# Seven block products in place of eight for the first MLP matrix, in three of four chunks of a decoder layer

## The chip, the cores and the metric

The kernel runs on one core of one Trainium2 chip. The metric is the device time of one execution in microseconds; the time before is the median of three runs. The engines are called by the profile's names: PE (TensorE, matmuls; PEld are its weight loads), DVE (VectorE), ACT (ScalarE), POOL (GpSimd) and SP (SyncE, which here only issues DMAs). DMAs are issued by SP, ACT or POOL, each in the order of its own queue.

## The reference

One decoder layer on 512 tokens of width 1024, in float32: a normalised input, a token mixer (gated linear attention and latent attention side by side, merged by gates and projected), a layer norm, an MLP of hidden width 4096 with squared ReLU, and a last layer norm. The change lies in the MLP and in what feeds it:

```python
h = layer_norm(x, ln_in_g, ln_in_b)
for l in range(DEPTH):          # DEPTH = 1
    mix = token_mixer(h, ...)
    h = layer_norm(DEEPNORM_ALPHA * h + mix, ln1_g[l], ln1_b[l])
    ff = jnp.square(jax.nn.relu(h @ w_ff1[l])) @ w_ff2[l]     # (512,1024)@(1024,4096), (512,4096)@(4096,1024)
    h = layer_norm(DEEPNORM_ALPHA * h + ff, ln2_g[l], ln2_b[l])
```

## The kernel before

**Precision.** Every large product is made of three matmuls. An operand is split into a high part in the matmul's own rounded format and a low part, the rest; the kernel adds high x high, high x low and low x high. A split is one ACT copy (the high part) and one DVE subtraction (the low part). Weights are split on the chip after loading: `pump` (lines 157 to 184) walks one list, `stream`, of weight tiles of 128 x 1024 in the order in which they are needed, issues their loads on SP two entries ahead and their splits (lines 180 and 181) one entry ahead, for the second MLP product two ahead.

**The MLP.** The hidden width is handled in four chunks (`FC`) of 1024. In each chunk the first product runs `gemm_fm` (lines 221 to 244) over blocks of hidden features: a weight block of 128 x 128 is stationary, 512 tokens move, over eight k blocks; in all 8 x 8 x 3 = 192 matmuls of 512 columns. In chunk 0 the first four feature blocks are done in two halves of 256 tokens, since the second half of the input is normalised later. `ev_h` (lines 1212 to 1224) takes the sums out of PSUM with a ReLU and a square on ACT and starts `win_hid` (lines 1104 to 1120), which makes the operands of the second product from a pair of feature blocks.

The second product, `win_f2` (lines 1122 to 1202), already uses the scheme of seven products (Strassen's in Winograd's form): both matrices are cut into quadrants, four sums of quadrants are formed on each side, and seven products of quadrants replace eight. In `WIN` (line 327) an item is a weight operand, a half of its k blocks and a phase 0 to 6; each item is 12 matmuls of 512 columns, so a chunk has 14 x 12 = 168. The weight operands are quadrants "11", "21", "22" and the sums T1 = 12 - 11, T3 = 22 - 12, T2 = T3 + 11 and T4 = T2 - 21. `win_load` (line 1077) loads the quadrants of `w_ff2` through POOL's queue; `win_sums` (line 1086) makes T1, T3 and T2 on DVE, and T4 is made on DVE at line 1153. After the last item of a phase ACT copies the two banks out (line 1163), and POOL issues DMAs that add them to the residual rows in SBUF (line 1165). In chunk 3 the last six items run in another order, with their results added by DVE and the last layer norm following.

**Buffers and order.** Most tiles of 4 KB a partition share one pool `A` with 24 buffers; residual rows, T1 and T2 share eight others (tag C); `whi`/`wlo` have two each and `wraw` three; 2 KB tiles share pool `B` with 22. PSUM has four banks each in `pm` and `px`. The program is written as one main line with generators beside it (`spawn`, `tick`, `finish`), which are advanced between groups of matmuls. A scheduler then sets the order within each engine's queue by its own timing model; an engine runs its queue strictly in order, and a new tile waits until an old one of its pool is no longer used.

The input of the MLP is made by `ln_transpose` (lines 360 to 378): PE transposes, ACT writes the high part, DVE a temporary in pool `B` (line 368) and the low part. The result `h1T` is eight pairs of tiles (high, low) of 128 features x 512 tokens.

Of the kernel before, what the change touches and what calls it, by code (L numbers as in the profile page):

```python
# [10 lines left out]
F32 = mybir.dt.float32  # L11
# [5 lines left out]
ALU = mybir.AluOpType  # L17
# [35 lines left out]
def tile_hybrid_block(ctx: ExitStack, tc: tile.TileContext, I, out, dbg=None):  # L53
# [5 lines left out]
    sm = ctx.enter_context(tc.tile_pool(name="sm", bufs=4))  # L59
    pm = ctx.enter_context(tc.tile_pool(name="pm", bufs=4, space=bass.MemoryType.PSUM))  # L60
    px = ctx.enter_context(tc.tile_pool(name="px", bufs=4, space=bass.MemoryType.PSUM))

    uid = [0]
# [12 lines left out]
    def B(shape, dt=F32, n="b"):  # L76
        return pb.tile(shape, dt, tag="B", name=nm(n))
# [54 lines left out]


    stream = []
    st = {"dma": 0, "spl": 0, "gates": ()}
# [60 lines left out]
    def spawn(g):  # L196
        active.append(g)
        return g
# [122 lines left out]


    FC = 4
    F1 = [((0, 4), (4, 2), (6, 2))] + [tuple((b, 2) for b in range(0, 8, 2))] * 3
# [8 lines left out]
    fb = 0  # L333
    for ci in range(FC):
        nb = 8
        for b, w in F1[ci]:
            PL["f1", ci, b] = plan("w_ff1", (fb + b) * P, w * P, res=(ci == 0 and b == 0), per=8 // w)
        PL["f2", ci] = []
        for n, (op, hf, _) in enumerate(win_items(ci)):
            PL["f2", ci].append(len(stream))  # L340
            stream.append({"src": lambda q=(ci, op, hf): WQ[q], "nk": 2, "n": T, "res": False,
                           "ahead": 2, "home": "r" if ci == FC - 1 and n == 12 else HOMES[n]})
        fb += nb


    def ln_rows(src, dst, mv, on_act=False):
# [13 lines left out]
    def ln_transpose(rows, g, b, outs, hf, alt=False, n="h0"):  # L360
        tk = slice(hf * 256, (hf + 1) * 256)
        for k in range(NK):
            if len(outs) <= k:
                outs.append(A([P, 2, T], F32R, n) if n == "h0" else (B([P, T], F32R, n), B([P, T], F32R, n)))
            p = MM() if alt and k in (4, 5) else PX()
            for i in range(2):
                nc.tensor.transpose(p[:, i * P:(i + 1) * P], rows[2 * hf + i][:, k * P:(k + 1) * P], ident)
            tmp = B([P, 256], F32, "lnt")
# [9 lines left out]
            yield hd  # L378

    mvin = consts.tile([P, NT, 2], F32, name="mvin")  # L380
    hT = []

# [635 lines left out]
    finish(t_ln)  # L1018
    st["gates"] = st["ln"]
    t_ln = spawn(ln1(1))  # L1020
    accs = gemm_fm(PL["f1", 0, 0], h1T, T, None, toks=slice(0, 256))
    finish(t_ln)

    def residual1():
# [49 lines left out]
                nc.sync.dma_start(rows[:, c], r[:, c])  # L1074
        yield

    def win_load(ci):
        w2 = I["w_ff2"].rearrange("(k p) n -> p k n", p=P)
        for op, i, j in (("12", 0, 1), ("11", 0, 0), ("22", 1, 1), ("21", 1, 0)):
            for hf in range(2):  # L1080
                t = A([P, 2, T], F32, "wq")
                k0 = 8 * ci + 4 * hf + i
                nc.gpsimd.dma_start(t, w2[:, k0:k0 + 3:2, j * T:(j + 1) * T])
                WQ[ci, op, hf] = t

    def win_sums(ci):
        def held(*a, **kw):
            with ExitStack() as gates:
                if "ev" in st:
                    gates.enter_context(tc.issue_after(st["ev"].ins))  # L1090
                vtt(*a, **kw)
        for hf in range(2):
            q12 = WQ.pop((ci, "12", hf))
            t1 = WQ[ci, "T1", hf] = A([P, 2, T], F32, "T1")
            held(t1, q12, WQ[ci, "11", hf], op=ALU.subtract)
            yield
            held(q12, WQ[ci, "22", hf], q12, op=ALU.subtract)
            WQ[ci, "T3", hf] = q12
            yield
            t2 = WQ[ci, "T2", hf] = A([P, 2, T], F32, "T2")  # L1100
            held(t2, q12, WQ[ci, "11", hf], op=ALU.add)
            yield

    def win_hid(R, ops):
        a11, a12, a21, a22 = R[:, 0, :256], R[:, 1, :256], R[:, 0, 256:], R[:, 1, 256:]
# [16 lines left out]
    def win_f2(ci, hid):  # L1122
# [20 lines left out]
            return o  # L1143

        for n, (op, hf, ph) in enumerate(items[:8] if end else items):
            pump(PL["f2", ci][n])
# [4 lines left out]
            if n in (5, 6):  # L1151
                t2, q21 = WT.pop((ci, n - 5))
                vtt(t2, t2, q21, op=ALU.subtract)
                WQ[ci, "T4", n - 5] = t2
            if end and n == 6:
                gb.extend([bcast_row("ln2_g"), bcast_row("ln2_b")])
                for tt in range(3):
                    nc.sync.dma_start(out[tt * P:(tt + 1) * P, :], gb[1])
            if hf == 1:
                for t in range(2):  # L1160
                    o = bank[{3: 0, 6: 0, 5: 2}.get(ph, ph), t]
                    e = B([P, T], F32, "ev")
                    st["ev"] = act(e, o, AF.Copy, scale=-1.0 if ph == 4 else 1.0)  # L1163
                    for tt, j in (((0, 0),), ((0, 0),), ((2, 1),), ((0, 1),), ((2, 0),), ((0, 1),), ((2, 0), (2, 1)))[ph]:
                        nc.gpsimd.dma_start(res[tt + t][:, j * T:(j + 1) * T], e, accum_op=ALU.add)  # L1165
            if n == 9 and not end:
                win_load(ci + 1)
        if not end:
            return

# [31 lines left out]
        finish(spawn(ln2(3, bst)))  # L1202

    gb = []
    WQ, WT = {}, {}
    for ci in range(FC):
        nb = 8
        hid = []
        if ci == 0:
            win_load(0)  # L1210

        def ev_h(a, ps):
            r = B([P, T], F32, "relu")
            act(r, ps, AF.Relu)  # L1214
            if a % 2 == 0:
                hid.append({"R": A([P, 2, T], F32, "hr")})
            ops = hid[-1]
            R = ops["R"]
            act(R[:, a % 2, :], r, AF.Square)
            if a % 2:  # L1220
                h1 = A([P, 2, 2, 256], F32R, "h1p")
                split(R[:, :, :256], h1[:, 0], h1[:, 1])
                ops[0], ops[1] = [(h1[:, 0, i], h1[:, 1, i]) for i in range(2)]
                spawn(win_hid(R, ops))
        for b, w in F1[ci]:
            if ci == 0 and b == 0:
                gemm_fm(PL["f1", ci, b], h1T, T, ev_h, toks=slice(256, T), accs=accs)
                t_r1 = spawn(residual1())
            else:
                gemm_fm(PL["f1", ci, b], h1T, w * P, ev_h, width=2)  # L1230
            if b == 0:
                t_ws = spawn(win_sums(ci))
        if ci == 0:
            finish(t_r1)
        finish(t_ws)
        for hf in range(2):
            WT[ci, hf] = (WQ[ci, "T2", hf], WQ[ci, "21", hf])
        win_f2(ci, hid)


# [46 lines left out]
```

## Time and profile before

| what | value |
|---|---|
| time, median of 3 runs | 903.64 us (902.91 to 904.17) |
| span of the profiled execution | 901.4 us |
| instructions | 11,728 |
| PE matmuls | 4,472 |
| bytes moved by DMA | 101.47 MB |

The profiled execution is one of its own beside the three runs; the profile gives its span, from the first to the last instruction. Busy times are by engine, and the page's list of costliest groups merges instructions of one line. A matmul's duration in the list (389 ns for 512 columns) contains its latency, in which the next one already runs; how often matmuls follow one another is read from a window's length and their number.

### The profile page before, as it was taken

The page shows a single profiled execution, that of the slowest core. Times are in us where ns is not written, and L with a number is a line of the kernel's source. Part 1 is how long each engine was busy: PE and PEld are TensorE (multiplying, and loading weights), DVE is VectorE, ACT ScalarE, POOL GpSimd, SP SyncE. Part 2 cuts the span into 40 slices and gives each one's busy share as a digit, 9 for nine tenths or more (in the row PEclk, how much of TensorE's full clock was granted, in tenths as well). Part 3 has the DMA queues.
Part 4 walks back from the last instruction along what each step waited for, and adds up shares of the span by engine and source line. Part 5 has one row for each costly group of instructions (what it writes and reads, how often), then busy time and mean ns, then how long its engine had stood idle before and what let it go on. Part 6 is the DMA issues. An engine that isn't in the chain of part 4 may idle for free.

```text
span 901.4 us, 11728 instructions
## 1 busy us (share of the span) xinstructions
PE 878.1 (97%) x4472; PEld 746.5 (83%) x4472; DVE 566.1 (63%) x919; ACT 439.8 (49%) x745; POOL 172.8 (19%) x203
## 2 busy tenths in 40 slices
PE   5999999999999999999999999999999999999994
PEld 5988888888888888888888888988888888888883
DVE  7835855575635244657756797997557656754666
ACT  5555443444434333435645423366357546645654
POOL 1003442442511010000000002104400520241032
PEclk9999999999999999999999999999999999999997
DMA  7413213212213332212207618005940990397084
GB/s 243 122 47 94 90 52 94 71 47 71 75 38 93 88 105 74 68 42 65 94 24 260 205 49 303 2 0 139 302 120 25 261 249 25 80 312 169 1 210 94
DMA packets 63335, 101.47 MB, mean 113 GB/s; under 512 B 7680, under 2 KB 31616, under 8 KB 63280
## 3 DMA queue, kind: packets, MB, share of 16 engines
q1 hardware_dynamic: 48256, 64.04, 22.7%
q0 software_dynamic: 13104, 33.04, 15.2%
q10 hardware_dynamic: 1920, 3.66, 1.2%
q8 instruction: 35, 0.57, 0.3%
q14 instruction: 20, 0.16, 0.1%
HBM read 82.36 MB, written 3.67 MB: 95 GB/s over the span
## 4 chain that ended last, share of the span: by engine, by line
PE 92%; DMA 2%; ACT 2%; POOL 1%; issue 1%; DVE 1%; POOLq 0%; DVEq 0%; ACTq 0%
PE mm L231 16%; PE mm L233 15%; PE mm L232 15%; PE mm L264 6%; PE mm L265 6%; PE mm L266 6%; PE px L1141 3%; PE px L1140 3%; PE px L1142 3%; PE mm L1141 2%; PE mm L1140 2%; PE mm L1142 2%; PE px L680 2%; DMA res<-ev 1%; PE px L837 1%
## 5 line engine op out<-in xcount | busy, mean ns | idle before, releaser
L181 DVE TENSOR_TENSOR wlo<-wraw,whi 128x1024 fp32r<-128x1024 f32 (+1 forms) x104 | 117.7, 1132 | 162.3 <-ACT whi L180 154.9
L231 PE MATMUL mm<-h,whi 128*128 128x512 f32 x416 | 162.6, 392 | 0.4 <-ACT gt L924 0.4
L232 PE MATMUL mm<-h,whi 128*128 128x512 f32 x416 | 162.4, 390 | 0.0
L180 ACT ACTIVATE whi<-wraw 128x1024 fp32r<-128x1024 f32 (+1 forms) x104 | 100.3, 964 | 118.7 <-PE mm L232 68.3
L233 PE MATMUL mm<-h,wlo 128*128 128x512 f32 x416 | 154.9, 390 | 0.0
L1165 POOL DMA_DIRECT2D res<-ev x56 | 48.6, 980 | 238.2 <-ACT ev L1163 195.8
L231 PEld LDWEIGHTS mm<-h,whi 128*128 128x128 f32 x416 | 78.1, 188 | 16.3 <-ACT gt L924 0.6
L233 PEld LDWEIGHTS mm<-h,wlo 128*128 128x128 f32 x416 | 77.9, 188 | 16.4 <-DVE wlo L181 0.3
L232 PEld LDWEIGHTS mm<-h,whi 128*128 128x128 f32 x416 | 78.2, 188 | 15.6
L265 PE MATMUL mm<-wlo,h 128*128 128x512 f32 x128 | 50.3, 393 | 0.0
L266 PE MATMUL mm<-whi,h 128*128 128x512 f32 x128 | 50.1, 392 | 0.0
L264 PE MATMUL mm<-whi,h 128*128 128x512 f32 x128 | 49.7, 403 | 0.0
L1214 ACT ACTIVATE relu<-mm 128x512 f32<-128x512 f32 x32 | 18.8, 595 | 56.8 <-PE mm L233 56.8
L352 POOL TENSOR_TENSOR mv<-mv,mhalf 128x1 f32<-128x1 f32 x4 | 4.6, 1154 | 211.7 <-DVE mv L351 211.7
L619 POOL TENSOR_TENSOR rp<-rp 128x256 f32<-128x256 f32 x32 | 31.4, 983 | 60.9 <-ACT E L624 44.1
L626 DVE TENSOR_TENSOR M<-E,qk 128x512 f32<-128x512 f32 x32 | 27.3, 853 | 16.5 <-ACT E L624 16.5
L624 ACT ACTIVATE E<-rp 128x512 f32<-128x512 f32 x32 | 20.4, 638 | 26.9 <-POOL rp L620 26.9
L180 ACT ACTIVATE xh<-wraw 128x1024 fp32r<-128x1024 f32 (+1 forms) x20 | 19.0, 959 | 24.7 <-PE mm L266 16.0
L181 DVE TENSOR_TENSOR wlo<-wq,whi 128x1024 fp32r<-128x1024 f32 x15 | 18.4, 1223 | 19.7 <-ACT whi L180 19.7
L620 POOL TENSOR_TENSOR rp<-rp 128x256 f32<-128x256 f32 x32 | 27.5, 860 | 10.3 <-ACT q L649 8.1
L266 PEld LDWEIGHTS mm<-whi,h 128*128 128x128 f32 x128 | 24.0, 188 | 5.0
L265 PEld LDWEIGHTS mm<-wlo,h 128*128 128x128 f32 x128 | 24.1, 188 | 4.3
(383 smaller groups left out, 2240.9 us busy)
## 6 DMA issues: line engine op xcount, KB each, us to landing
wraw<-in_w_in_dram SPq DMA_DIRECT2D x40, 512.0 KB, 3.5
wraw<-in_w_ff_dram SPq DMA_DIRECT2D x32, 512.0 KB, 7.6
wq<-in_w_ff_dram POOLq DMA_DIRECT2D x32, 512.0 KB, 9.4
res<-ev POOLq DMA_DIRECT2D x56, 256.0 KB, 8.3
wraw<-in_w_o_gla_dram SPq DMA_DIRECT2D x8, 512.0 KB, 3.7
wraw<-in_w_o_mla_dram SPq DMA_DIRECT2D x8, 512.0 KB, 3.2
wraw<-in_w_out_dram SPq DMA_DIRECT2D x8, 512.0 KB, 4.3
wraw<-in_w_in_dram SPq DMA_DIRECT2D x8, 360.0 KB, 5.1
```

The source lines that it names most:

```text
L180: st["ins"] = act(hi[:, :nk, :n], raw[:, :nk, :n], AF.Copy)
L181: vtt(lo[:, :nk, :n], raw[:, :nk, :n], f(hi[:, :nk, :n]), op=ALU.subtract)
L231: mm(o, hi[:, c], xh, start=first, stop=False)
L232: mm(o, hi[:, c], xl, start=False, stop=False)
L233: mm(o, lo[:, c], xh, start=False, stop=last)
L264: mm(o, xh, hi[:, :n], start=opens, stop=False, skip_group_check=share)
L265: mm(o, xh, lo[:, :n], start=False, stop=False, skip_group_check=share)
L266: mm(o, xl, hi[:, :n], start=False, stop=last, skip_group_check=share)
L1140: mm(o, xh[:, c], hi[:, pp, cols], start=opens, stop=False, skip_group_check=True)
L1141: mm(o, xh[:, c], lo[:, pp, cols], start=False, stop=False, skip_group_check=True)
L1142: mm(o, xl[:, c], hi[:, pp, cols], start=False, stop=hf == 1 and pp == 1, skip_group_check=True)
L1165: nc.gpsimd.dma_start(res[tt + t][:, j * T:(j + 1) * T], e, accum_op=ALU.add)
```

## The change

The first product of chunks 1 to 3 is made by the same scheme of seven products. The weight `w_ff1` of a chunk is cut in quadrants by k and by features, the input in quadrants by k and by tokens. Where the second product's weight pieces had been taken in every other k block, chunks 1 to 3 now take them in the order in which the first product leaves the hidden features.

- `win_f1` (new) runs 14 items in the order 11, T1, T2, 21, T3, 22, T4, each of 24 matmuls of 256 columns, with weights stationary and tokens moving. Three pairs of banks hold the sums; in between ACT copies them to four tiles `R` (`copy`), DVE adds (`add`), and ACT applies ReLU and square to whole quadrants (`relu2`, `tail`). `put` splits quadrants into operands for the second product; `tail` forms their four sums. Two of the operands are written over parts of `h1T` that are no longer read.
- `sums_h1` (new) forms the four sums of the input's quadrants once, during the second product of chunk 0, and splits them; they stay in eight tiles. For this `ln_transpose` keeps its temporaries in tiles of 128 x 1024 and SP stores them to DRAM (`H1D`), from where they are read again.
- `load` replaces `win_load` after chunk 0 and issues all weight quadrants on SP; `hooks` places loads and sums at given items.
- `wsum` makes the weight sums, T2 and T4 in place. T1 and T3 of the first product stay on DVE; T2 and T4 of the first product and all four of the second go to POOL (`gtt`), each a tensor of 128 x 1024. Chunk 0 keeps its own on DVE, without the wait for an evacuation that `held` gave them.
- Splits of weight tiles go round three places (`"rww"`), for the first product two items ahead as well.

```diff
-    TAG_C = ('h0', 'qn', 'PT1', 'res', 'bc', 'T1', 'T2')
+    TAG_C = ('h0', 'qn', 'PT1', 'res', 'bc', 'T1', 'T2', 'w21')
...
+    WIN1 = tuple((op, hf, ph) for op, ph in (("11", 0), ("T1", 2), ("T2", 3), ("21", 1), ("T3", 6), ("22", 5), ("T4", 4))
+                 for hf in range(2))
...
+                home = "rww"[st["ring"] % 3] if u != ("f2", FC - 1) or n < 8 else "wawara"[n - 8]
...
+            if n == "h1":
+                if k % 4 == 0:
+                    raw = A([P, 4, 256], F32, "h1r")
+                tmp = raw[:, k % 4]
+            else:
+                tmp = B([P, 256], F32, "lnt")
...
+                if k % 4 == 3:
+                    H1D[hf, k // 4] = dr.tile([P, 4, 256], F32, name=nm("h1d"))
+                    nc.sync.dma_start(H1D[hf, k // 4], raw)
...
-                nc.gpsimd.dma_start(t, w2[:, k0:k0 + 3:2, j * T:(j + 1) * T])
+        (eng or nc.sync).dma_start(t, src[:, :, c0 + j * T:c0 + (j + 1) * T])
...
+    def wsum(u, op, hf, tt=None):
+        tt = tt or vtt
+        if op == "T1":
+            t = WQ[u, "T1", hf] = A([P, 2, T], F32, "T1")
+            tt(t, WQ[u, "12", hf], WQ[u, "11", hf], op=ALU.subtract)
...
+    for ci in range(1, FC):
+        u, v = ("f1", ci), ("f2", ci - 1)
+        for n, op, hf in ((6, "11", 0), (7, "11", 1), (8, "12", 0), (9, "12", 1), (10, "22", 0), (11, "22", 1)):
+            at(v, n, load, u, op, hf)
+        for hf in range(2):
+            at(u, 1 + hf, load, u, "21", hf)
+            at(v, 12 + hf, wsum, u, "T1", hf)
+            at(u, hf, wsum, u, "T3", hf)
+            at(u, 2 + hf, wsum, u, "T2", hf, gtt)
+            at(u, 6 + hf, wsum, u, "T4", hf, gtt)
+        v = ("f2", ci)
...
+        for hf in range(2):
+            at(u, 12 + hf, wsum, v, "T1", hf, gtt)
+            at(v, hf, wsum, v, "T3", hf, gtt)
+            at(v, 3 + hf, wsum, v, "T2", hf, gtt)
+            at(v, 5 + hf, wsum, v, "T4", hf, gtt)
...
+    def sums_h1():
+        q = {}
+        for i, j in ((1, 0), (1, 1), (0, 0), (0, 1)):
+            q[i, j] = A([P, 4, 256], F32, "h1q")
+            nc.sync.dma_start(q[i, j], H1D[i, j])
+        yield
...
+        vtt(q[1, 1], q[1, 0], q[1, 1], op=ALU.add)
+        yield
+        put(2, q[1, 1])
...
+    def win_f1(ci, hid):
...
+            for pp in range(2):
+                k = 2 * hf + pp
+                xh, xl = x(ph, k, 0), x(ph, k, 1)
+                for m in range(4):
...
+                    mm(o, hi[:, pp, c], xh, start=first, stop=False, skip_group_check=True)
+                    mm(o, hi[:, pp, c], xl, start=False, stop=False, skip_group_check=True)
+                    mm(o, lo[:, pp, c], xh, start=False, stop=k == 3, skip_group_check=True)
+                tick(4)
...
+        def tail():
+            for t in range(2):
+                r = R[2][:, 2 * t:2 * t + 2]
+                act(r, bank[0, t].rearrange("p (a b) -> p a b", b=256), AF.Relu)
+                act(r, r, AF.Square)
+                yield
...
+            s1 = A([P, 4, 256], F32, "hr")
+            vtt(s1, R[2], R[3], op=ALU.add)
+            put(2, s1)
...
+    at(("f2", 0), 7, lambda: spawn(sums_h1()))
+    win_f2(0, hid)
+    for ci in range(1, FC):
+        hid = [{} for _ in range(4)]
+        win_f1(ci, hid)
         win_f2(ci, hid)
```

More of the change, by code (lines that the diff above doesn't have):

```diff
@@ L323, in tile_hybrid_block @@
     FC = 4
-    F1 = [((0, 4), (4, 2), (6, 2))] + [tuple((b, 2) for b in range(0, 8, 2))] * 3
+    F1 = ((0, 4), (4, 2), (6, 2))
     HOMES = "wwrawarawawawa"
@@ L1075, in ln2 @@
         yield
-    def win_load(ci):
-        w2 = I["w_ff2"].rearrange("(k p) n -> p k n", p=P)
-        for op, i, j in (("12", 0, 1), ("11", 0, 0), ("22", 1, 1), ("21", 1, 0)):
-            for hf in range(2):
-                t = A([P, 2, T], F32, "wq")
-                k0 = 8 * ci + 4 * hf + i
-                nc.gpsimd.dma_start(t, w2[:, k0:k0 + 3:2, j * T:(j + 1) * T])
[L1084 to L1091, printed above, removed]
+    WQ = {}
@@ new lines, in load @@
+    def load(u, op, hf, eng=None):
+        what, ci = u
+        i, j = int(op[0]) - 1, int(op[1]) - 1
+        t = A([P, 2, T], F32, "w21" if op == "21" and ci else "wq")
+        if what == "f1":
+            src, c0 = I["w_ff1"].rearrange("(k p) n -> p k n", p=P)[:, 4 * i + 2 * hf:4 * i + 2 * hf + 2], 8 * ci * P
+        else:
+            w2 = I["w_ff2"].rearrange("(k p) n -> p k n", p=P)
+            k0 = 8 * ci + (4 * i + 2 * hf if ci else 4 * hf + i)
+            src, c0 = w2[:, k0:k0 + 2] if ci else w2[:, k0:k0 + 3:2], 0
+        (eng or nc.sync).dma_start(t, src[:, :, c0 + j * T:c0 + (j + 1) * T])
+        WQ[u, op, hf] = t
@@ L1092, in win_sums, with at, hooks, win_load0 @@
+    HOOKS = {}
+    def at(u, n, fn, *args):
+        HOOKS.setdefault((u, n), []).append((fn, args))
+    def hooks(u, n):
+        for fn, args in HOOKS.pop((u, n), ()):
+            fn(*args)
+    def win_load0():
+        for op in ("12", "11", "22", "21"):
+            for hf in range(2):
+                load(("f2", 0), op, hf, nc.gpsimd)
+    def win_sums0():
+        u = ("f2", 0)
         for hf in range(2):
-            q12 = WQ.pop((ci, "12", hf))
-            t1 = WQ[ci, "T1", hf] = A([P, 2, T], F32, "T1")
@@ L1204, in tile_hybrid_block, with ev_h @@
     gb = []
[L1205 to L1237, printed above, removed]
+    hid = []
+    win_load0()
+    def ev_h(a, ps):
+        r = B([P, T], F32, "relu")
+        act(r, ps, AF.Relu)
+        if a % 2 == 0:
+            hid.append({"R": A([P, 2, T], F32, "hr")})
+        ops = hid[-1]
+        R = ops["R"]
+        act(R[:, a % 2, :], r, AF.Square)
+        if a % 2:
+            h1 = A([P, 2, 2, 256], F32R, "h1p")
+            split(R[:, :, :256], h1[:, 0], h1[:, 1])
+            ops[0], ops[1] = [(h1[:, 0, i], h1[:, 1, i]) for i in range(2)]
+            spawn(win_hid(R, ops))
+    for b, w in F1:
+        if b == 0:
+            gemm_fm(PL["f1", b], h1T, T, ev_h, toks=slice(256, T), accs=accs)
+            t_r1 = spawn(residual1())
+            t_ws = spawn(win_sums0())
+        else:
+            gemm_fm(PL["f1", b], h1T, w * P, ev_h, width=2)
+    finish(t_r1)
+    finish(t_ws)
+    at(("f2", 0), 7, lambda: spawn(sums_h1()))
+    win_f2(0, hid)
+    for ci in range(1, FC):
+        hid = [{} for _ in range(4)]
+        win_f1(ci, hid)
         win_f2(ci, hid)
```

171 lines of the change are left out of this document (146 added, 25 removed).

## The prediction

> **What bounds the kernel now.** I read the page first, then stretches of time cut where the MLP's loops begin and end (taken from the lines of the matmuls), then the groups by line and shape, then POOL in order of time.
>
> ```profile
> PE 878.1 (97%) x4472; PEld 746.5 (83%) x4472; DVE 566.1 (63%) x919; ACT 439.8 (49%) x745; POOL 172.8 (19%) x203
> ...
> PE 92%; DMA 2%; ACT 2%; POOL 1%; issue 1%; DVE 1%; POOLq 0%; DVEq 0%; ACTq 0%
> ```
>
> PE is busy 97% of the span and carries 92% of the chain that ended last. The windows of the MLP (time, then busy us and instructions of PE, PEld, DVE, ACT, POOL, clock, DMA share, GB/s) alternate between second product and first product, from the second product of chunk 0:
>
> ```profile
> 605.33:643.41 38.08, 38.08 (x170) 31.54 (x169) 28.22 (x29) 23.04 (x32) 14.50 (x18) 1.00 0.68 196
> 643.41:686.93 43.52, 43.52 (x194) 36.05 (x193) 22.77 (x31) 23.07 (x34) 5.18 (x6) 1.00 0.51 119
> 686.93:725.01 38.08, 38.08 (x170) 31.54 (x169) 27.01 (x27) 21.95 (x31) 14.40 (x18) 1.00 0.70 198
> 725.01:768.53 43.52, 43.52 (x194) 36.05 (x193) 22.93 (x31) 23.81 (x35) 5.15 (x6) 1.00 0.50 117
> 768.53:806.61 38.08, 38.08 (x170) 31.54 (x169) 27.24 (x28) 23.27 (x32) 14.39 (x18) 1.00 0.72 203
> 806.61:850.13 43.52, 43.52 (x194) 36.05 (x193) 22.71 (x31) 22.47 (x33) 5.17 (x6) 1.00 0.48 113
> ```
>
> PE never pauses, at the full granted clock of 1.00. A first product of 192 matmuls of 512 columns takes 43.52 us (0.2267 each), a second of 168 takes 38.08; a chunk takes 81.6. DVE has a third of each window to spare, POOL two thirds. So a gain has to come from fewer PE columns, and it lasts only while the other engines keep up.
>
> **PE's new count.** Seven products of four k blocks, four feature blocks and three passes are 7 x 4 x 4 x 3 = 336 matmuls of 256 columns in place of 192 of 512: 86,016 columns for 98,304. The trace has such matmuls in the first stage of chunk 0:
>
> ```profile
> 558.50:568.50 10.00, 10.00 (x86) 1.00 0.43 151
> ...
> 575.30:586.00 10.70, 10.70 (x82) 10.29 (x81) 10.67 (x14) 3.87 (x8) 0.00 (x0) 1.00 0.01 2
> ```
>
> In the first row (PE alone) 86 matmuls, the outermost two in part, lie in 10.00 us: 0.116 to 0.119. In the second, all engines, 82 lie in 10.70: 0.130, with DVE busy for all but 0.03 us and PE now and then behind it. I take 0.120. So 336 x 0.120 = 40.3 us: 3.2 us less per first product, not the 5.4 that an eighth of 43.52 would be; at 0.116 it is -4.5, at 0.130 +0.2. Three chunks: -9.6. That is the whole expected gain. Chunk 0's first product stays.
>
> **What DVE and ACT pay.** Rows by line and shape, from the second product of chunk 0 to the last:
>
> ```profile
> L181 DVE TENSOR_TENSOR wlo<-wraw,whi 128x1024 fp32r<-128x1024 f32 x24 | 29.4, 1225 | 48.0 <-ACT whi L180 48.0
> ...
> L1091 DVE TENSOR_TENSOR T<-wq,wq 128x1024 f32<-128x1024 f32 x12 | 14.4, 1220 | 0.9 <-DMA wq<-in_w_ff_dram 0.9
> ...
> L107 DVE TENSOR_TENSOR h1p<-hr,h1p 128x512 fp32r<-128x512 f32 x12 | 8.2, 684 | 0.0
> ...
> L107 DVE TENSOR_TENSOR a<-hr,a 128x256 fp32r<-128x256 f32 x12 | 5.0, 418 | 0.0
> L180 ACT ACTIVATE whi<-wraw 128x1024 fp32r<-128x1024 f32 x26 | 27.4, 1055 | 10.1 <-PE mm L1142 5.7 <-PE mm L232 4.1
> L1163 ACT ACTIVATE ev<-px 128x512 f32<-128x512 f32 x30 | 17.3, 596 | 17.2 <-DMA res<-ev 11.6 <-PE px L1142 2.7 <-PE mm L1142 2.6
> ```
>
> A full-tile two-input DVE operation costs 1.22 us, a half tile 0.68, a quarter 0.42; a full-tile ACT pass 1.055.
> First product, changed chunk, DVE: 14 low parts of weights (8 before) 17.1; two T3 sums 2.4; the split of the first quadrant 4 x 0.42 = 1.7 and of the second 1.2; six additions from PSUM 4.1. Sum 26.5 of 40.3 us.
> Second product, DVE: 14 low parts 17.1; two T1 sums of the next chunk 2.4; four hidden sums of `tail` 4.9; four full-tile splits 4.9 and one in quarters 1.7. Sum 31.0 of 38.1. The old splits and sums of `win_hid` go away.
> ACT per chunk: 28 weight passes 29.5, 18 full tiles' worth of copies, ReLU, squares and high parts about 19, 14 evacuations of 0.6: 58 of 78.4 us. It stays below PE, as does DVE by itself.
>
> **What POOL pays, and what that costs DVE.** Per changed chunk POOL does twelve 128x1024 sums: T2, T4 and the next product's T1 (two halves each) in the first product, T3, T2 and T4 in the second. The trace has none of 1024 columns. The nearest are these, with the two DVE operations beside them (first the instructions of a line with min/median/max in ns, then rows of the timeline):
>
> ```profile
> L535 POOL TENSOR_TENSOR g<-g,az x4: 1298/1307/2343, 66.7 to 71.5; 128x512 f32<-128x512 f32 x4
> L620 POOL TENSOR_TENSOR rp<-rp x32: 613/760/1605, 97.6 to 250.6; 128x256 f32<-128x256 f32 x32
> 66.67 6.11 POOL L535 TENSOR_TENSOR g<-g,az 128x512 f32<-128x512 f32 x4 [40.71 <-ACT az L532]
> 69.14 1.23 DVE L181 TENSOR_TENSOR wlo<-wraw,whi 128x1024 fp32r<-128x1024 f32 x1 [6.57 <-ACT whi L180]
> 71.53 2.33 DVE L181 TENSOR_TENSOR wlo<-wraw,whi 128x1024 fp32r<-128x1024 f32 x1 [1.17 <-ACT whi L180]
> ```
>
> Undisturbed, 256 columns take 0.61 and 512 take 1.30, so 1024 take 1.30 + 2 x 0.69 = 2.67, or 2.60 as two of 512. I take 2.6. The last rows matter more. Four POOL operations of 1.30 would be 5.2 us; they took 6.11, since one of them took 2.34 while a DVE subtraction ran; and the next subtraction took 2.33 where it takes 1.23, over the last 1.1-1.2 us of the fourth POOL operation. They ran one after the other, whichever came first, not side by side. So a POOL sum isn't taken off DVE: where DVE has two SBUF operands, it holds DVE for 2.6 us in place of the 1.22 that DVE itself would need.
>
> The Trainium skill has this as a rule (SBUF — State Buffer, "SBUF: two separate sides"): the port pair that DVE and GpSimd share is an exclusive lock kept for a whole instruction, also against DVE operations with two SBUF inputs. The trace agrees by the 2.33 us. By the Trainium skill's GPSIMD Engine Reference, section 3.1 (4497 ns for 2048 columns), a sum would be an estimated 2.25 us, which would take about 2 us off each second product's excess below.
>
> So DVE's two-SBUF work and POOL's sums are added (PSUM additions may lie beside a POOL sum):
> First product: 22.4 + 6 x 2.6 = 38.0 of 40.3 us: fits, barely.
> Second product: 31.0 + 15.6 = 46.6 of 38.1 us: 8.5 too long. Weights are split at most two items ahead (5.4 us), so little can be moved out. Bounds: nothing, if POOL's sums only fall in DVE's pauses, to +8.5 plus what imperfect packing adds. That DVE can be packed shows here:
>
> ```profile
> 557.70:568.70 11.00, 11.00 (x93) 10.95 (x93) 10.89 (x21) 2.13 (x3) 3.12 (x2) 1.00 0.47 165
> ```
>
> 10.89 of 11.00 busy. I add 1.0 per chunk for packing (bounds 0 and 4, about 5% of 86).
>
> **POOL's queue.** POOL still issues 14 accumulating DMAs per chunk, in order, and a sum behind one that waits is late. POOL by time, at the end of a second product and in the next:
>
> ```profile
> 646.71 0.84 POOL L1165 DMA_DIRECT2D res<-ev  x1 [6.64 <-DMA res<-ev]
> 648.42 4.34 POOL L1165 DMA_DIRECT2D res<-ev  x5 [0.87 <-DMA res<-ev]
> 695.95 1.72 POOL L1165 DMA_DIRECT2D res<-ev  x2 [43.19 <-ACT ev L1163]
> 702.32 0.84 POOL L1165 DMA_DIRECT2D res<-ev  x1 [4.65 <-ACT ev L1163]
> 703.63 0.85 POOL L1165 DMA_DIRECT2D res<-ev  x1 [0.48 <-DVE wlo L181]
> ...
> 728.62 1.72 POOL L1165 DMA_DIRECT2D res<-ev  x2 [7.17 <-DMA res<-ev]
> ```
>
> The last accumulations of a second product left 3.6 to 5.3 us into the next first product (728.62 and 730.34 less 725.01), those of the one before until 9.35 us into it (648.42 + 4.34 - 643.41). T2 is queued behind them. Its second half would be ready 5.3 + 2 x (2.6 + 1.22) = 12.9 or 17.0 us in, with one DVE operation before each; item 5 begins 5 x 2.88 = 14.4 in and needs ACT's and DVE's 2.3 us before, so 12.1. That is 0.8 to 4.9 late; I take 2.5 per chunk.
>
> **The rest.** Chunk 0's second product gets four sums and four splits of the hidden input (`sums_h1`: 8 x 1.22 = 9.8 DVE, 4.2 ACT), with its 28.22 DVE about 38.0 of 38.08; T1 replaces sums that stood there. Two of them can slip into the next chunk. I take +2 (0 to +6, if half doesn't fit). The `w_ff2` loads move from POOL's queue to SP's, eight per chunk, so SP issues 16 loads a chunk, in order; a load that waits for a buffer holds up the `w_ff1` quadrants behind it. The input's way to DRAM and back is four stores and four reads of 512 KB, covered by the DMA shares of 0.5 to 0.7 and by being issued seven items ahead; a load of that size lands in 7.6 us:
>
> ```profile
> wraw<-in_w_ff_dram SPq DMA_DIRECT2D x32, 512.0 KB, 7.6
> ```
>
> Without that cover a product waits for such a landing. I cost it at nothing (0 to +4). In the LN stage only the buffer of the temporary changes (0 to +2).
>
> **Sum.** Chunks 1 and 2: -3.2 + 2.5 + 8.5 + 1.0 = +8.8 each. Chunk 3 has no next T1 (8.5 - 2.4 = 6.1), and about 7 us of PE follow its last split, which I let cover 2: -3.2 + 2.5 + 4.1 = +3.4. Chunk 0: +2. In all 17.6 + 3.4 + 2 = +23.0 on the profiled span of 901.4: 924.4. The median of the runs, 903.64, lies 2.2 above that span, so 926.6, say 926.
>
> **The rivals.**
> *PE's count decides* (chance 0.14): POOL's sums mostly fall where DVE waits for ACT (48.0 us of such idle time stand in the L181 row), the ports don't meet, and DVE's 31.0 fits in 38.1. Then -9.6, at best -13.5: 894, at best 890. For it speaks DVE's idle third, against it the 2.33 us row and the 46.6. It decides if the shared load in a second product stays under 38.1 us, which takes POOL sums that block for less than (38.1 - 31.0) / 6 = 1.2 us each.
> *A near draw* (0.14): the lock holds, but half of the 8.5 us is placed in pauses of the first product and POOL isn't late: -3.2 + 4.2 = +1.0 a chunk, with chunk 0 about +2 to +5: 903 to 909. For it speaks the 2.3 us free in the first product.
> *POOL's order decides* (0.17): T2 is 4.9 late in each chunk, and T4 stands behind phase 1's accumulation, whose issue ended 704.48 - 686.93 = 17.6 us into the second product; its second half is ready at 17.6 + 7.6, split at 27.5, and item 9 begins at 24.5: 3.0 late. (8.5 - 3.2 + 4.9 + 3.0) x 3 + 2 = +41.6: 945. Against it: T4 may be placed before that issue.
> *Shared load decides*, my forecast, has 0.55; its own range is 911 to 938.
>
> **How the numbers follow.** The range 898 to 945 leaves out the most of the first rival (0.12) and the upper half of the third (0.08). What a measurement can tell from no change is about 0.2%, 1.8 us. Faster: 0.14 plus 0.02 of the draw = 0.16; same 0.04 of the draw; slower 0.80.
>
> **What would show it.** First products without a stall take 40.3 us; 43 or more says that T2 or the ring of three splits is late. Second products of 45 to 48 us with PE waiting for DVE's low parts, those at means well over 1.22 us and POOL sums over 2.6, show the shared load. DVE rows at 1.22 beside POOL sums, and second products at 38.1, would make the forecast wrong; 256-column matmuls at 0.130 without a stall would take the gain away by themselves. POOL sums whose idle time before them is ended by an accumulating DMA, with first products of 45 and more, show the third rival.

## The result and the profile after

| | before | after |
|---|---|---|
| time, median of the runs | 903.9 us (902.91 to 904.33) | 935.59 us (933.89 to 937.65) |
| ratio, 95% interval | | 1.0354 (1.0339 to 1.037) |
| span of the profiled execution | 901.4 us | 935.9 us |
| PE matmuls | 4,472 | 4,904 |

The change makes the kernel slower by 3.5%. The forecast was slower, 926 us with a range of its own from 911 to 938. The first and fourth part of the page after the change, busy times and the chain that ended last:

```profile
PE 884.0 (94%) x4904; PEld 765.0 (82%) x4904; DVE 635.1 (68%) x918; ACT 469.4 (50%) x770; POOL 267.3 (29%) x215
...
PE 70%; issue 10%; DVE 6%; DMA 5%; ACT 4%; POOL 3%; SPq 0%; POOLq 0%; DVEq 0%; ACTq 0%
```

PE carried 92% of the chain, now 70%. The windows after the change, cut at the first matmul of each product (columns as before: busy us of PE, PEld, DVE, ACT, POOL, clock, DMA share, GB/s). Second and first products alternate; the last row is what follows the last matmul.

```profile
608.99:654.01 45.02, 44.65 (x221) 37.65 (x220) 36.50 (x36) 31.60 (x43) 10.82 (x13) 1.00 0.83 210
654.01:697.53 43.52, 36.77 (x285) 36.15 (x284) 35.77 (x26) 23.47 (x29) 32.55 (x13) 0.92 0.42 122
697.53:743.57 46.04, 42.17 (x174) 32.97 (x173) 36.90 (x31) 27.94 (x39) 22.36 (x17) 0.96 0.67 160
743.57:783.40 39.83, 39.83 (x333) 39.82 (x332) 31.65 (x24) 24.16 (x31) 28.44 (x13) 1.00 0.46 133
783.40:830.63 47.23, 41.12 (x170) 32.22 (x169) 38.01 (x32) 29.39 (x41) 25.18 (x17) 0.96 0.66 156
830.63:871.84 41.21, 40.82 (x338) 40.41 (x336) 26.75 (x23) 26.53 (x34) 25.88 (x13) 1.00 0.45 128
871.84:919.10 47.26, 41.23 (x182) 32.86 (x180) 42.01 (x38) 30.14 (x47) 18.47 (x15) 0.96 0.49 110
919.10:935.90 16.80, 0.28 (x3) 0.07 (x1) 6.43 (x12) 2.70 (x5) 3.70 (x4) 0.61 0.52 98
```

Set against the windows of before (605.33 as the start, 38.08 and 43.52 in turn, 38.1 for the last second product, 13.1 behind its last matmul), the 34.5 us between the two spans lie here:

| stretch | change, us | forecast |
|---|---|---|
| up to chunk 0's second product (608.99) | +3.7 | 0 to +2 |
| chunk 0's second product | +0.7 | +2 |
| chunk 1, first and second product | +6.2, +8.0 | +8.8 together |
| chunk 2 | -3.7, +9.2 | +8.8 |
| chunk 3 | -2.3, +9.1 | +3.4 |
| behind the last matmul | +3.7 | 0 |

In the first window 52 matmuls of chunk 1's first product are already at work; at 0.12 us each, 6.2 us are counted there. The gain came as computed: first products of 39.83 and 41.21 in place of 43.52. Every second product gives back more than twice that, where PE needs 46 to 47 us for 38.1 us of matmuls. In those of chunks 2 and 3 PE's longest waits, 2.5 and 2.2 us, are for DVE's low parts, and these have grown. (In that of chunk 1 it is a sum of POOL that comes late; that case follows below.) Groups by line and shape, from 600 us on (columns as before):

```profile
L182 DVE TENSOR_TENSOR wlo<-wq,whi 128x1024 fp32r<-128x1024 f32 x42 | 72.3, 1724 | 37.4 <-ACT whi L181 37.4
...
L1122 POOL TENSOR_TENSOR wq<-wq,wq 128x1024 f32<-128x1024 f32 x12 | 37.9, 3157 | 41.0 <-DVE wlo L182 27.1 <-DVE wraw L182 12.0 <-PE px L1358 2.0
...
L1128 POOL TENSOR_TENSOR wq<-wq,w 128x1024 f32<-128x1024 f32 x6 | 23.5, 3928 | 0.3 <-DVE wlo L182 0.3
...
L1128 POOL TENSOR_TENSOR wq<-w,wq 128x1024 f32<-128x1024 f32 x6 | 16.2, 2700 | 4.4 <-DVE wlo L182 4.3
```

The low part's mean is 1.72 us where it was 1.22; POOL's sums take 2.7 to 3.9 in the mean. By itself such a sum takes about 2.40, the shortest (first) of the three times in these rows of the instructions by line:

```profile
L1122 POOL TENSOR_TENSOR wq<-wq,wq x12: 2392/3282/5526, 653.5 to 875.9; 128x1024 f32<-128x1024 f32 x12
...
L1128 POOL TENSOR_TENSOR wq<-w,wq x6: 2390/2404/3315, 666.0 to 841.8; 128x1024 f32<-128x1024 f32 x6
```

So both engines lengthen each other, as the prediction has it. But the mean hides that a few waits are far longer than one instruction of the other engine. The timeline of after, four places:

```profile
658.95 3.46 POOL L1378 DMA_DIRECT2D res<-ev  x4
660.12 5.75 DVE L182 TENSOR_TENSOR wlo<-wq,whi 128x1024 fp32r<-128x1024 f32 x1 [3.38 <-ACT whi L181]
661.16 3.62 POOL L1122 TENSOR_TENSOR wq<-wq,wq 128x1024 f32<-128x1024 f32 x1
...
665.93 0.58 PE L1296 MATMUL px<-sh,wlo 128*128 128x256 f32 x1 [5.05 <-DVE wlo L182]
...
668.01 0.41 PE L1295 MATMUL px<-sl,whi 128*128 128x256 f32 x1
668.23 0.41 PE L1296 MATMUL px<-sh,wlo 128*128 128x256 f32 x1
...
715.97 7.38 POOL L1128 TENSOR_TENSOR wq<-wq,w 128x1024 f32<-128x1024 f32 x2
...
723.37 2.01 ACT L181 ACTIVATE whi<-wq 128x1024 fp32r<-128x1024 f32 x2 [6.83 <-POOL wq L1128]
...
724.48 0.84 PE L1356 MATMUL mm<-whi,h 128*128 128x512 f32 x2 [2.43 <-ACT whi L181]
...
801.18 7.49 POOL L1128 TENSOR_TENSOR wq<-wq,w 128x1024 f32<-128x1024 f32 x1
...
804.08 2.34 DVE L108 TENSOR_TENSOR xl<-hr,xh 128x1024 fp32r<-128x1024 f32 x2
```

The low part of 660.12 needs 1.2 us and takes 5.75; PE waits 5.05 us for it, and then runs at little more than half its rate, one matmul in 0.21 us where it is 0.12 (granted clock 0.50 from 663.5 to 670.3). At 715.97 the two T4 sums of a second product come late: ACT waits 6.83 us for them to make high parts, and PE 2.43 us for ACT. At 801.18 it is POOL's turn: its sum takes 7.49 behind DVE operations that follow each other without a pause until 806.4.

POOL's DMA issues are not what lengthens a low part. From 608 us on, 26 full-tile low parts in weight splits ran beside such an issue and beside no sum, and none took more than 1.23 us; of the 35 beside a sum the longest is the 5.75.

### The profile page after: what moved, and what is told of

Same layout as the page of the kernel before. It is cut to its first block, busy times and chain, and to the rows that moved or that the text cites. A ratio compares the mean times of both kernels' runs of the same rounds, so it can differ in the third digit from the quotient of the medians.

```text
span 935.9 us, 12781 instructions
## 1 busy us (share of the span) xinstructions
PE 884.0 (94%) x4904; PEld 765.0 (82%) x4904; DVE 635.1 (68%) x918; ACT 469.4 (50%) x770; POOL 267.3 (29%) x215
## 4 chain that ended last, share of the span: by engine, by line
PE 70%; issue 10%; DVE 6%; DMA 5%; ACT 4%; POOL 3%; SPq 0%; POOLq 0%; DVEq 0%; ACTq 0%
PE mm L232 9%; PE mm L234 9%; PE mm L233 9%; PE mm L265 5%; PE mm L267 5%; PE mm L266 5%; DMA res<-ev 4%; PE px L1296 3%; PE px L1295 2%; PE px L1294 2%; DVE wlo L182 2%; PE px L700 2%; ACT whi L181 1%; POOL wq L1128 1%; DMA x<-in_x_dram 1%
## 5 line engine op out<-in xcount | busy, mean ns | idle before, releaser
L182 DVE TENSOR_TENSOR wlo<-wraw,whi 128x1024 fp32r<-128x1024 f32 (+1 forms) x80 | 88.2, 1104 | 116.4 <-ACT whi L181 109.0
L181 ACT ACTIVATE whi<-wraw 128x1024 fp32r<-128x1024 f32 (+1 forms) x80 | 74.9, 936 | 113.9 <-PE mm L233 67.0
L182 DVE TENSOR_TENSOR wlo<-wq,whi 128x1024 fp32r<-128x1024 f32 x42 | 72.3, 1724 | 37.4 <-ACT whi L181 37.4
L232 PE MATMUL mm<-h,whi 128*128 128x512 f32 x224 | 87.9, 394 | 0.4 <-ACT gt L944 0.4
L233 PE MATMUL mm<-h,whi 128*128 128x512 f32 x224 | 87.7, 391 | 0.0
L234 PE MATMUL mm<-h,wlo 128*128 128x512 f32 x224 | 83.1, 391 | 0.0
L1378 POOL DMA_DIRECT2D res<-ev x56 | 48.8, 1024 | 115.6 <-ACT ev L1376 96.8
L181 ACT ACTIVATE whi<-wq 128x1024 fp32r<-128x1024 f32 x42 | 44.2, 1055 | 33.6 <-POOL wq L1128 10.2
L1122 POOL TENSOR_TENSOR wq<-wq,wq 128x1024 f32<-128x1024 f32 x12 | 37.9, 3157 | 41.0 <-DVE wlo L182 27.1
L232 PEld LDWEIGHTS mm<-h,whi 128*128 128x128 f32 x224 | 42.1, 188 | 8.9 <-ACT gt L944 0.6
L234 PEld LDWEIGHTS mm<-h,wlo 128*128 128x128 f32 x224 | 41.8, 188 | 8.8 <-DVE wlo L182 0.3
L233 PEld LDWEIGHTS mm<-h,whi 128*128 128x128 f32 x224 | 42.1, 188 | 8.2
L182 DVE TENSOR_TENSOR wraw<-wq,wraw 128x1024 fp32r<-128x1024 f32 x20 | 34.1, 1707 | 3.1 <-PE px L1357 2.9
L181 ACT ACTIVATE xh<-wraw 128x1024 fp32r<-128x1024 f32 (+1 forms) x20 | 18.7, 954 | 24.8 <-PE mm L267 16.0
```

The lines of the kernel that those rows point to most:

```text
L181: st["ins"] = act(hi[:, :nk, :n], raw[:, :nk, :n], AF.Copy)
L182: vtt(lo[:, :nk, :n], raw[:, :nk, :n], f(hi[:, :nk, :n]), op=ALU.subtract)
L232: mm(o, hi[:, c], xh, start=first, stop=False)
L233: mm(o, hi[:, c], xl, start=False, stop=False)
L234: mm(o, lo[:, c], xh, start=False, stop=last)
L1122: tt(t, WQ[u, "T3", hf], t, op=ALU.add)
```

## The experiments

All times are medians; before measured 903.5 to 903.9 beside them.

**All sums on DVE.** Every `gtt` of the placed sums falls away:

```diff
-            at(u, 2 + hf, wsum, u, "T2", hf, gtt)
+            at(u, 2 + hf, wsum, u, "T2", hf)
```

> The 36 sums that POOL makes are made by DVE, nothing else. Theory S (a POOL sum and a DVE operation with two SBUF operands exclude one another): each sum costs DVE 1.22 us instead of a hold of 2.4 us and more, so DVE's work in a second product is 31.0 + 6 x 1.22 = 38.3 us for PE's 38.1; second products fall from 46-47 to 39-42 us, no low part of a weight takes over 1.3 us, and the time is 912 to 920 us. Rival L (DVE's own work is what is too much, and POOL does relieve it): twelve more sums of 1.22 us per chunk make it 14 us per chunk worse, 945 us or more.

Measured: 926.47 us (925.37 to 927.26), 1.0252 (1.0236 to 1.0267), between what the two theories expected. It is 9 us better than with POOL, and no low part of the MLP's weights is longer than 1.23 any more; but the second products take 47.8, 47.3 and 44.3 us. The first of them whole, and its first half (windows), then the timeline behind that half:

```profile
686.88:734.69 47.81, 41.88 (x171) 33.63 (x170) 37.27 (x36) 29.51 (x41) 10.22 (x12) 0.93 0.64 154
687.00:711.00 24.00, 21.47 (x88) 17.22 (x87) 22.92 (x23) 19.04 (x28) 5.10 (x6) 0.93 0.40 84
```

```profile
715.67 1.23 DVE L1116 TENSOR_TENSOR T<-wq,wq 128x1024 f32<-128x1024 f32 x1 [3.15 <-DMA wq<-in_w_ff_dram]
...
722.43 1.23 DVE L1119 TENSOR_TENSOR wq<-wq,wq 128x1024 f32<-128x1024 f32 x1 [2.64 <-DMA wq<-in_w_ff_dram]
723.57 1.22 DVE L182 TENSOR_TENSOR wlo<-wq,whi 128x1024 fp32r<-128x1024 f32 x1
```

DVE is full in the first 24 us and then waits for quadrants to land, with a weight split queued behind the waiting sum. The sums are dear on DVE as well, through their place in the queue.

**The sums' reads taken away.** POOL sums 4 of each 512 columns and, in the second kernel, writes the rest twice without reading, so that it is occupied about as long (the out-of-place sums fill their tile once in the first kernel):

```diff
+    def tiny(o, a, b, op):
+        gtt(o[:, :, :4], a[:, :, :4], b[:, :, :4], op=op)
+        for _ in range(2):
+            nc.gpsimd.memset(o[:, :, 4:], 0.0)
```

> POOL's sums are made over 4 of each 512 columns only (a new T1 tile is filled up with zeros by POOL), so that the places in the queues and the dependences stay, and the sums' time is nearly nothing; the weights of the changed chunks are therefore other numbers. Theory S: second products of 38 to 41 us and 905 to 914 us in all. Rival L: DVE's own 57.6 us per chunk still bind; second products stay at 45 us or more and the time above 930 us.

> As with the tiny sums, but POOL then also fills the rest of each result with zeros twice, about 2 us that write SBUF and read none; the weights of the changed chunks are other numbers. POOL is as occupied as in the changed kernel. Theory S, with SBUF reads as what excludes: DVE's low parts stay at 1.22 us and the time is within 5 us of the run with tiny sums, 905 to 917 us. Rival Q (POOL's queue is late, because it has too much to do in order): the time stays at 930 us or more. If writes exclude DVE as well, low parts of 2 us and more appear and the time lies at 925 us or more.

Measured: 912.73 (one run) and 910.9 us (909.33 to 911.53), 1.0077 (1.0062 to 1.0093). Of the second, two groups, and the windows of the three second products:

```profile
L1142 POOL MEMSET wq<- 128x1016 f32 x60 | 62.7, 1059 | 5.1 <-ACT ev L1381 3.7 <-issue 0.8
L182 DVE TENSOR_TENSOR wlo<-wq,whi 128x1024 fp32r<-128x1024 f32 x42 | 51.2, 1222 | 43.3 <-ACT whi L181 43.2
...
687.10:731.31 44.21, 41.30 (x175) 33.13 (x173) 32.43 (x32) 28.39 (x39) 19.86 (x24) 0.96 0.69 167
771.14:812.11 40.97, 39.14 (x170) 31.22 (x169) 32.64 (x31) 27.31 (x39) 21.77 (x23) 1.00 0.73 177
852.42:892.88 40.46, 38.69 (x181) 31.88 (x180) 33.23 (x37) 28.88 (x45) 15.74 (x20) 1.00 0.56 128
```

POOL's queue has the same order as in the changed kernel and writes for 2 x 1.06 us in place of each sum, and low parts are back at 1.22. It is the reading sums that cost, 935.6 - 910.9 = 24.7 us, and not POOL's order. By the windows some 15 us of this lie in the second products and some 10 in the first ones, nearly all of these in chunk 1 (34.11 for 43.52). But even so the kernel is slower than before, and its second products still take 40.5 to 44.2 us. One of their waits fits the order: in the first of them PE again waits 2.47 us for a high part of T4, as in the changed kernel.

**Half of the sums moved.** Second products' sums (T3, T2, T4) to DVE, or the sums placed in the first products:

```diff
-            at(v, 3 + hf, wsum, v, "T2", hf, gtt)
+            at(v, 3 + hf, wsum, v, "T2", hf)
```

> Only the sums that are placed in the second products (T3, T2, T4 of the second matrix) go to DVE; those placed in the first products stay on POOL. Theory S: second products as with all sums on DVE, 39 to 42 us; first products as in the changed kernel, 40 to 43.5 us; 912 to 922 us, since the load in a first product just fits. Rival Q: first products lose as much to POOL as second ones did, and little more than half of the gain of all sums on DVE is left: 925 us.

> The mirror of the fourth run: the sums placed in first products go to DVE, those in second products stay on POOL. Theory S with DVE's sum as the bound: second products keep their 46 to 47 us, first products lose the two long stalls of chunk 1; 927 to 931 us. Rival P (it is POOL's sums in the first products alone that cost, since moving the others changed 1.5 us): 924 to 927 us, as with all on DVE.

| sums in first products on | in second products on POOL | on DVE |
|---|---|---|
| POOL | 935.6 | 934.1 (932.7 to 935.4) |
| DVE | 922.2 (920.1 to 923.4) | 926.5 |

Taking POOL out of the first products gains 13.4 or 7.6 us. In the second products POOL costs 1.5 us beside POOL in the first, which is within the scatter, and saves 4.3 otherwise. Of these 4.3, 3.9 lie behind the last matmul (16.9 us in the profile with all sums on DVE, 13.0 here), so within the second products it makes little difference which engine sums. The stall of 660 to 666 us remains in the one (PE waits 5.06) and is gone in the other. Both kernels missed both of their expectations, the first from above (934.1 for 912 to 925) and the second from below: none had POOL's sums cost less in the second products than in the first.

**The input's copy.** Temporaries of the last transposes stay in the small pool, nothing is stored, and rows of `x` are read in place of the stored input (the sums of the input are then of other numbers):

```diff
-            nc.sync.dma_start(q[i, j], H1D[i, j])
+            nc.sync.dma_start(q[i, j], I["x"][(2 * i + j) * P:(2 * i + j + 1) * P, :].rearrange("p (k t) -> p k t", t=256))
```

> The input's temporaries stay in the small pool and are not stored to DRAM; the four tiles that are read back hold rows of x instead, so the sums of the input are other numbers. The second product of chunk 0 began at 609.0 us in the changed kernel and 605.3 before. If the larger temporaries and their stores are the cause, it begins at 605 to 606 and the time falls by 2 to 4 us to 932 to 934; if the scheduler's new order or the sums' new places are, it stays at 608 to 609 and 935 us.

Measured: 933.76 us (930.48 to 935.54), 1.0326 (1.0304 to 1.0349). Chunk 0's second product begins at 606.0 in place of 609.0; of these 3 us the end keeps some 1.8, within the scatter.

**POOL in the kernel before.** The kernel before, with its eight sums per chunk on POOL:

```diff
-                vtt(*a, **kw)
+                gtt(*a, **kw)
...
-                vtt(t2, t2, q21, op=ALU.subtract)
+                gtt(t2, t2, q21, op=ALU.subtract)
```

> The kernel before, with its eight weight sums per chunk moved from DVE to POOL, nothing else. Theory S: DVE's 50 us per chunk less 9.8 and plus 8 x 2.4 for which POOL holds it are 59 of 81.6 us; low parts beside a sum take up to 3.6 us, but there is room: 903 to 912 us. Rival R (a POOL sum costs its hold whatever room DVE has): 32 x (2.4 - 1.2) = +38, 940 us.

Measured: 923.83 us (923.55 to 924.75), 1.0223 (1.0206 to 1.024): between the two. Second products stay at 38.08, first products grow from 43.52 to between 46.64 and 47.67, the start loses 8 us and the end 2. By the sum of the work DVE has room for all of it there. Its timeline at 659 us:

```profile
659.27 10.56 DVE L181 TENSOR_TENSOR wlo<-wraw,whi 128x1024 fp32r<-128x1024 f32 x2 [5.02 <-ACT whi L180]
659.48 5.17 POOL L1091 TENSOR_TENSOR T<-wq,wq 128x1024 f32<-128x1024 f32 x2
...
665.30 3.44 POOL L1091 TENSOR_TENSOR wq<-wq,wq 128x1024 f32<-128x1024 f32 x1
```

The first of two low parts waits for two POOL sums in a row, until 664.65, the second for the next one, until 668.74: 8.1 us of waiting in 10.56. From 640 us on PE waits five times for such a low part, 5.9 us in all. So here it isn't the sum of the work, it is the latency of single splits.

**Smaller pieces.** If the engine that waits got the port after each instruction of the other, sums in four pieces of 256 columns would cost a low part one piece at most, 0.6 us by the prediction's row. First all of POOL's sums, then, with the first products' sums on DVE and every sum queued behind the last weight split, those of the second products:

```diff
+    def quarters(o, a, b, op):
+        for i in range(2):
+            for c in (slice(0, 256), slice(256, T)):
+                gtt(o[:, i, c], a[:, i, c], b[:, i, c], op=op)
...
-            at(u, 2 + hf, wsum, u, "T2", hf, gtt)
+            at(u, 2 + hf, wsum, u, "T2", hf, quarters)
```

> Each of POOL's 36 sums is made in four instructions of 128x256 in place of one of 128x1024; POOL's time is the same, 4 x 0.61 us. In the changed kernel a single low part of a weight took up to 5.75 us, over more than one POOL sum. Theory F (the port changes hands after each instruction): a low part waits at most one quarter, none takes over 2.5 us, and the time falls to 915 to 925 us. Rival K (POOL keeps the port while its next sum stands ready): low parts of 4 us and more remain and the time is 931 to 938 us.

> The sums placed in first products on DVE, queued behind the splits as in the run with that order; those placed in second products on POOL, in quarters. By theory F, POOL's six sums of a second product hold DVE for no longer than DVE's own six would have taken in pieces of 0.61 us, and DVE is relieved where it is fullest: 908 to 915 us. By rival K, the long waits come back in the second products: 918 to 924 us.

Measured: 945.05 us (943.45 to 945.98), 1.0461 (1.0444 to 1.0478), the slowest of all and above both expectations, and 935.24 us (934.0 to 935.82), 1.0347 (1.0332 to 1.0363). The timeline of the first:

```profile
664.14 7.23 POOL L1142 TENSOR_TENSOR wq<-w,wq 128x256 f32<-128x256 f32 x8
...
667.28 7.28 DVE L182 TENSOR_TENSOR wraw<-wq,wraw 128x1024 fp32r<-128x1024 f32 x1
...
670.71 4.41 POOL L1142 TENSOR_TENSOR T<-wq,wq 128x256 f32<-128x256 f32 x4
```

One DVE operation of 1.2 us takes 7.28, while POOL gets through more than four quarter sums. So the port, as the prediction calls what the two engines take turns at, doesn't change hands after each instruction: POOL, with its next sum ready, kept it, and cutting the sums didn't let DVE in. The first products of chunks 1 and 3 suffer most there, the latter takes 49.6 us. In the second kernel, slower than both theories had it, the second products take 48.7, 49.0 and 52.2 us; in the first two of them PE's longest waits, 5.0 and 4.4 us, are for high parts of the hidden operands and not for low parts of weights.

**Sums on DVE, in a better order.** All on DVE, and each placed sum queued right behind the last weight split:

```diff
+                st["lo"] = vtt(lo[:, :nk, :n], raw[:, :nk, :n], f(hi[:, :nk, :n]), op=ALU.subtract)
...
+            if fn is wsum:
+                with tc.issue_after(st["lo"].ins):
+                    fn(*args)
```

> All sums on DVE as in the first run, and each placed sum queued behind the last weight split that was issued before it. With all sums on DVE, a low part stood behind a sum that waited up to 2.6 us for its quadrant to be loaded, and PE stalled 3.2 to 3.6 us there, twice. If this order is what was left, those two stalls and the slower clock after them go: 917 to 922 us. If DVE's amount of work is, the stalls move to later products and the time stays at 925 to 929 us.

Measured: 915.73 us (914.92 to 916.38), 1.0131 (1.0115 to 1.0146). A little under the expected range, the fastest version that leaves nothing out, and still slower than before.

**What is left.** The same without the input's copy, and, in the other kernel, no copy and all sums of chunks 1 to 3 over 4 columns on DVE:

```diff
+    def tiny(o, a, b, op):
+        if o is not a and o is not b:
+            nc.gpsimd.memset(o[:, :, 4:], 0.0)
+        vtt(o[:, :, :4], a[:, :, :4], b[:, :, :4], op=op)
...
-            at(v, 12 + hf, wsum, u, "T1", hf)
+            at(v, 12 + hf, wsum, u, "T1", hf, tiny)
```

> All sums on DVE, queued behind the last weight split as before, and in addition no copy of the input through DRAM (x rows are read back in its place, so the products use other numbers). If start and sums add: 915.7 less 2 to 3 us, 912.5 to 914. If the start's gain is lost in the next wait: 915 to 916.

> All weight sums of chunks 1 to 3, DVE's T1 and T3 of the first product too, are made over 4 of each 512 columns on DVE, so the products use other numbers; the temporaries of the last transposes stay in the small pool and x rows are read back in place of the stored input. Theory S (the sums' time in the shared port and on DVE, and the copy, are all that the change pays beside its gain): the first products give back 3 x 3.2 to 3.7 us, the start loses at most 1 us, second products come to 38.1 to 39.5, the end is 3.2 longer: 895 to 901. Rival W (second products also wait for things that are no sum: a quadrant's landing, ACT's high parts, three copies of the ring): second products of 40 us and more as in the run with memsets, 905 to 909.

Measured: 911.83 us (910.7 to 913.6), 1.0089 (1.0074 to 1.0104): 3.9 less than with the copy, a little more than expected; chunk 0's second product begins at 604.5 in place of 608.4. And 909.23 us (908.97 to 911.4), 1.0058 (1.0041 to 1.0074): a shade above the range of other waits. The second kernel's windows, of a whole second product and of 5 us pieces inside it, and the DVE timeline:

```profile
684.57:732.82 48.25, 41.02 (x173) 33.20 (x171) 28.74 (x36) 28.52 (x39) 12.26 (x14) 0.93 0.63 153
...
710.00:715.00 5.00, 5.00 (x24) 4.14 (x23) 1.30 (x2) 3.18 (x4) 1.74 (x2) 1.00 1.09 301
715.00:720.00 5.00, 3.09 (x14) 2.24 (x12) 0.17 (x1) 3.20 (x4) 1.75 (x2) 1.00 1.09 306
720.00:725.00 5.00, 0.00 (x0) 0.00 (x0) 1.06 (x2) 0.00 (x0) 0.00 (x0) 0.81 1.00 231
```

```profile
723.93 0.17 DVE L1133 TENSOR_TENSOR wq<-wq,wq 128x8 f32<-128x8 f32 x1 [6.44 <-DMA wq<-in_w_ff_dram]
724.04 1.23 DVE L181 TENSOR_TENSOR wlo<-wq,whi 128x1024 fp32r<-128x1024 f32 x1
```

With the sums nearly gone, the next wait shows: the eight quadrant loads issued within one second product, beside its accumulations, fill the DMA engines (share 1.0 to 1.09). A quadrant lands late, DVE waits 6.44 us for it, the weight split behind it is late, and PE stalls for 7.2 us. That the loads are late because the engines are full fits these rows, but no run spread the loads out to test it. In the changed kernel itself this wait is covered by the others (5.4 us in all before its T1 sums).

## Why the prediction was right, and where its terms were off

- *PE's count.* 0.120 us a matmul and 40.3 a first product held: 39.83 in chunk 2 (some matmuls lie in the window before), and 40.31 in both whole first products of the run with sums behind splits and no copy.
- *The shared load decides.* It is the largest term, shown by the run with writes in place of sums: the reading sums are 24.7 us of the changed kernel. Their own price was 2.40 us, not 2.6. But that the time fell into the range is in part luck. In the second products the shared load was counted at 8.5, 8.5 and 4.1 us and is worth some 15 by that run, and the run still lies 17 us above the 894 that PE's count alone was to give. Waits that the forecast had at little or nothing (T4, quadrants, the start, the end) made up for it.
- *Second product 46.6.* Measured 46.04, 47.23, 47.26. The size was right, but the reason is only half of it: with POOL free of sums, DVE's 31.0 + 6 x 1.22 = 38.3 us fill 38.08 too, and the product takes 47.81; with neither engine reading for these sums it still takes 40.5 to 44.2. The alternative of DVE was not worked out.
- *First product "fits, barely", T2 2.5 late.* Here the step failed that a sum holds DVE for its own 2.6 us. In chunk 1's PE was idle for 43.52 - 36.77 = 6.75 us, most of it in the wait of 5.05, and some 1.7 us went to matmuls at the lower clock; chunk 2's lost nothing, chunk 3's 0.9. The table of halves puts 7.6 to 13.4 us on the first products.
- *Copy and temporaries at nothing (0 to +4; 0 to +2).* They cost 3.9 us in the one pair of runs where nothing covers it, within the bounds but not nothing. In the start 24 matmuls that stood ahead of the transposes come after them; the transposes wait for DVE twice, 0.91 and 0.35 us, and the granted clock then is 0.5 for 3.4 us. With all sums on DVE the order and the waits are the same, that slow stretch is missing, and chunk 0's second product begins at 606.9 in place of 609.0. Which of the two edits, pool or copy, brings the order wasn't separated.
- *Chunk 3 at +3.4 and the end at nothing.* They measured +6.8 and +3.7. Chunk 3's second product loses 9.1 us, as much as chunk 2's: neither the 2.4 us for the T1 that it doesn't make nor the cover of 2 us for the last splits shows. (The packing of 1.0 was also left out of this chunk's sum.) Behind its last matmul the changed program takes 13.26 us without sums and copy and 13.0 with POOL's sums in the second products alone, as before, and 15.4 to 17.4 in the other runs. So it is no fixed cost of the change; which operation sets it stays open.
- *The rivals.* "PE's count decides" falls twice: the load isn't under 38.1 us, and with hardly any load of sums the kernel still takes 909, with waits for quadrants. A near draw falls by the time, and by the place: the first products, which were to take up half of the excess, bear POOL least. "POOL's order decides" falls by the memsets, and T2 late in each chunk doesn't show (first products of 39.83 and 41.21). But its term for T4 came much as written: in chunk 1 the issue of the accumulation ended 18.7 us into the second product and the second sum 25.8 (17.6 and 25.2 in the prediction), and PE waited 2.43 us. The forecast had no such term.
- *Two sums.* ACT's terms (29.5, 19 and 14 x 0.6) add up to 57 us, not 58, and three chunks at +1.0 with chunk 0's +2 put the near draw at 909, with no term that gives its 903. The forecast rests on neither.

## What to carry to other kernels

Before work is moved to POOL, ask whether both its operands and those of the DVE work beside it come from SBUF. If so, the two took turns here, and what counts is the longest wait of one DVE operation that PE needs next, not the mean. Keeping such sums on DVE and queueing them behind the operation on which PE waits was better here (926.5 to 915.7); in one arrangement alone, whole sums in the second products only, POOL's sums did no harm (922.2 against 926.5, most of it behind the last matmul). And a gain of 7% in one of two alternating stages is lost if the preparation for it fills the other: here 9 to 10 us of PE time were bought with sums, splits, copies and loads that each had their own next wait.

## What the runs showed of the hardware

- POOL and DVE, each reading two operands from SBUF, took turns, and the turn didn't change after each instruction. An engine with its next one ready kept it: a low part of 1.22 us took about 6.5 behind two sums in a row, another operation 7.28 behind quarter sums; a POOL sum of 2.40 took 7.49 behind DVE. In the case of 5.75 us POOL's records of four DMA issues and of the sum overlap, so what the sum alone held isn't resolved there.
- POOL operations that only write, 72 memsets of 1,016 columns, left DVE's low parts at 1.22 us. DVE's additions that read PSUM stayed at 0.68 us in the changed kernel, seven of them beside a POOL sum. POOL's DMA issues left low parts at 1.23 us or less.
- After a stall of 5 us PE ran matmuls of 256 columns in 0.213 us instead of 0.120, 18 of them, about 1.7 us more; the granted clock was 0.50 from 663.5 to 670.3 us.
- A DMA share of 1.0 to 1.09 at 231 to 306 GB/s held for 15 us, and quadrants of 512 KB then landed 5 to 7 us apart.
